# A two-layer decoder trunk on one core: first token loads on ScalarE's queue, squares folded on GpSimd to one product per chunk, and the norm-factor multiply placed behind one weight split

## The chip, the core and the metric

The kernel runs on one core of one Trainium2 chip. A core has five engines with a queue of instructions each, taken strictly in order: TensorE (PE, with its weight loads shown as PEld), VectorE (DVE), ScalarE (ACT), GpSimd (POOL) and SyncE (SP). SP does no arithmetic; it issues DMAs, and so can ACT and POOL. The engines meet only through semaphores. The metric is device time in microseconds for one execution, of which a profile shows one.

## What is computed

Two layers over 256 tokens of width 1024. Each layer is an attention sub-layer followed by a gated ConvFFN, each behind an RMSNorm and added to the residual. Layer 1 mixes three dilated windows (three groups of 16 heads of 64), layer 2 is block-sparse attention, which over 256 tokens is one causal block.

```python
def rmsnorm(x, gain):
    y = xf * lax.rsqrt(jnp.mean(xf * xf, axis=-1, keepdims=True) + RMS_EPS)
    return y * gain

# attention: q and k are normalised per head before rope
q = apply_partial_rope(rmsnorm(qkv[:, :, 0], q_gain), cos, sin)
k = apply_partial_rope(rmsnorm(qkv[:, :, 1], k_gain), cos, sin)
# layer i:
hn = rmsnorm(x, attn_norm[i]); x = x + mixer(hn)
hn = rmsnorm(x, ffn_norm[i]);  x = x + conv_ffn(hn)
```

All inputs are float32. The answer is the sum after the second layer, float32.

## The kernel before

**Tiles and numbers.** Tokens stand in two chunks of 128 (c = 0, 1). A product of float32 precision is made of three products of shortened operands (`mm3`, lines 374 to 376): high part by high part, low by high, high by low. Tokens are split once per norm into `xT` (high and low), weights are split when they arrive.

**The weight stream** (`Stream`, lines 49 to 112). Weights come in units of 512 KB (`raw`, four buffers, loaded by SP). `start` makes the high part of a unit on ACT (`whi`, line 83), `finish` the low part on DVE (`wlo`, line 92) and then issues the load that takes the freed `raw` buffer. The first four units are split in two halves.

**Turns** (line 175). The whole kernel is a list of turns. A turn issues, in this order: `start` for a unit; what stands in the table `first` for this turn; one `finish`; what stands in `pre`; the other `finish`es; the turn's own products on PE, with what stands in `mid` issued half way; what stands in `post`. The call `at(table, dt, fn, ...)` (line 172) enters work for a turn `dt` later. Each engine executes its instructions in the order in which they were issued, so these tables set every engine's order; no scheduler changes it (line 124).

**The first attention.** A `qk_block` for one head group has four parts of 12 products of 512 columns: (c 0, first half of the depth), (c 0, second half), (c 1, first), (c 1, second). In the first section, turns 0 to 3 are the first group's, taken as c 0, c 1, c 0, c 1 (line 651): turns 0 and 1 use units 0 and 1, turns 2 and 3 units 2 and 3, turns 4 and 5 (the second group, c 0) units 4 to 7. When a chunk's part is done, ACT evicts it twice (`sq`, `qk`, lines 422 and 423). One turn later `head_sums` runs: DVE sums the squares by head, POOL makes the factor `rs_y` (`rsqrt_pool`, lines 251 and 253), DVE applies rope. One turn after that `factors` multiplies `qk` by `rs_y` on DVE (line 449), and one turn later PE transposes `qk` (line 465). Attention itself is a chain of steps in later turns: scores on PE (`step_A`), `step_E` (DVE line 582, ACT exponentials line 592), `step_R` (DVE lines 599 and 602 divide `sm`), `step_T` (PE transposes of `sm`, line 609), `step_C` (PE, line 631). A section is four heads of each group; there are four sections.

**The first norm** (`FirstNorm`, line 322). The tokens come already transposed (`x_t`), so the sum of squares over the width runs over partitions. ACT squares two halves of 512 columns, one engine adds the halves (POOL for chunk 0, DVE for chunk 1, line 343), and `sums` (line 345) adds 512 columns by four 128x128 products with a column of ones on PE, which ACT copies to `rn_s` (line 349) and POOL turns into `rn_e` (line 310). `rn_e` goes into every `rs_y` of the chunk.

**The start of the program** (lines 198 to 245 and 820 to 864). SP issues, in this order: `gn` (the gains), half a chunk of tokens, units 0 and 1, two more halves, unit 2, the last half, unit 3, then `pk` (308 KB of packed small tables), then the further units as buffers come free. `gain_tables` (line 231) is 16 small instructions on POOL that read `pk`; it is entered for `post` of turn 0.

Of the kernel before, what the change touches and what calls it, by code (L numbers as in the profile page):

```python
# [17 lines left out]
P = 128  # L18
# [97 lines left out]
def trunk_kernel(ctx, tc, x, a_w_qkv, a_w_o, b_w_qkv, b_w_o, ffn_norm, ffn_w_up, ffn_w_down, gains, pack, mask_a, mask_b,  # L116
                 x_t, out):
    nc = tc.nc
# [51 lines left out]
    first, pre, mid, post = {}, {}, {}, {}  # L170

    def at(table, dt, fn, *args):
        table.setdefault(now[0] + dt, []).append((fn, args))
# [21 lines left out]
        nc.gpsimd.dma_start(g, ffn_norm[l:l + 1, :].to_broadcast([P, D]))  # L195
        return g

    def load_T(c, h):
        nc.sync.dma_start(x_T[c][:, h * 512:(h + 1) * 512], x_t[:, c, h * 512:(h + 1) * 512])

    gn = cp.tile([P, 2, 8], F32, name="gn")
    nc.sync.dma_start(gn, gains.rearrange("p (l k) -> p l k", l=2))
    x_T = [xr[:, c, :] for c in range(2)]
    load_T(0, 0)
    ident = cp.tile([P, P], F32, name="ident")
    make_identity(nc, ident)
    ones = cp.tile([P, 1], F32, name="ones")
    nc.gpsimd.memset(ones, 1.0)
    mhalf = cp.tile([P, 2 * HS], F32, name="mhalf")
    nc.gpsimd.memset(mhalf, -0.5)  # L210
    ws.load(2)
    load_T(1, 0)
    load_T(0, 1)
    ws.load(3)
    load_T(1, 1)
    ws.load(4)


# [29 lines left out]
    def rsqrt_pool(ssq, scale, eps, keep=None):  # L248
        n = ssq.shape[-1]
        v = sp.tile([P, 2 * HS], F32, name="rs_v", bufs=2)[:, 0:n]  # L250
        nc.gpsimd.tensor_scalar(v, ssq, scale, eps, op0=ALU.mult, op1=ALU.add)  # L251
        y = sp.tile([P, 2 * HS], F32, name="rs_y", bufs=4)[:, 0:n] if keep is None else keep
        nc.gpsimd.tensor_tensor(y, v, mhalf[:, 0:n], op=ALU.pow)  # L253
        return y


    class Norm:
# [4 lines left out]
        def square(self, h):  # L262
            junk = sp.tile([P, 512], F32, name="sq", bufs=2)
            nc.scalar.activation(junk, xr[:, self.c, h * 512:(h + 1) * 512], AF.Square,
                                 accum_out=self.acc[:, h:h + 1])
# [56 lines left out]
    class FirstNorm(LateNorm):  # L322
# [15 lines left out]
        def square(self, h):  # L338
            sq = bp.tile([P, 512], F32, name="qk", bufs=4)
            nc.scalar.activation(sq, self.src[:, h * 512:(h + 1) * 512], AF.Square)  # L340
            self.sq.append(sq)
            if h == 1:
                (nc.gpsimd, nc.vector)[self.c].tensor_add(self.sq[0], *self.sq)

        def sums(self):
            acc = ps.tile([P, 512], F32, name="S", bufs=2)[:, 0:1]
            for k in range(4):
                nc.tensor.matmul(acc, self.sq[0][:, k * P:(k + 1) * P], ones, start=(k == 0), stop=(k == 3))
            nc.scalar.activation(self.ssq, acc, AF.Copy)
            self.offset()  # L350

# [27 lines left out]
    def attention(xT, norms, ng, g0, mask):  # L379
# [36 lines left out]
        def qk_block(g, res, rq):  # L416
            res.append(None)

            def done(c, acc):
                qk = bp.tile([P, 512], F32, name="qk", bufs=4)  # L420
                sq = sp.tile([P, 512], F32, name="sq", bufs=2)
                nc.scalar.activation(sq, acc, AF.Square)  # L422
                nc.scalar.activation(qk, acc, AF.Copy)
                at(first, 1, head_sums, c, qk, sq)

            def head_sums(c, qk, sq):
                ssq = sp.tile([P, 8], F32, name="qssq", bufs=2)
                nc.vector.tensor_reduce(ssq, sq.rearrange("p (h d) -> p h d", d=HD), axis=AX.X, op=ALU.add)  # L428
                rs = rsqrt_pool(ssq, 1.0 / HD, norms[c].eps)

                t4 = qk.rearrange("p (j h d) -> p j h d", j=2, d=HD)
                ra = sp.tile([P, 2, HS, 16], F32, name="ra", bufs=1)
                rb = sp.tile([P, 2, HS, 16], F32, name="rb", bufs=1)
                cg = CG[:, c, g0 + g]
                sg = SG[:, c, g0 + g]
                nc.vector.tensor_mul(ra, t4[:, :, :, 0:16], cg[:, :, None, :].to_broadcast([P, 2, HS, 16]))
                for lo_, hi_ in ((0, 8), (8, 0)):
                    nc.vector.tensor_mul(rb[:, :, :, lo_:lo_ + 8], t4[:, :, :, hi_:hi_ + 8],
                                         sg[:, :, None, lo_:lo_ + 8].to_broadcast([P, 2, HS, 8]))
                nc.vector.tensor_add(t4[:, :, :, 0:16], ra, rb)  # L440
                at(first, 1, factors, c, qk, rs)

            def factors(c, qk, rs):

# [199 lines left out]
        for sec in range(NSEC):  # L644
            qk, v, rq = [], [None, None], {}
# [176 lines left out]
    norms = [FirstNorm(xT, c, gn[:, 0], x_T[c], ssq[:, c:c + 1]) for c in range(2)]  # L822
# [10 lines left out]
    def unit():  # L833
        ws.start(1)
        ws.finish(1)
# [7 lines left out]
    norms[0].split(2, 2)  # L843
    unit()
    norms[1].split(0, 4)
    for h in range(2):
        norms[0].square(h)
    norms[0].split(4, 4)

    def second_halves():  # L850
        unit()
        norms[1].split(4, 4)
        unit()
        for h in range(2):
            norms[1].square(h)

    at(post, 0, gain_tables)
    at(mid, 1, second_halves)
    at(mid, 2, norms[0].sums)
    at(mid, 3, norms[1].sums)  # L860
    at(post, 6, factors)
    at(post, 6, nc.sync.dma_start, mA, mask_a)
    at(post, 20, nc.sync.dma_start, mB, mask_b)
# [113 lines left out]
```

## Time and profile before

| | |
|---|---|
| median of 3 runs | 798.68 us (797.98 to 798.79) |
| the profiled execution | 798.67 us, of which the span of the core's instructions is 796.9 us |
| busy | PE 784.2, PEld 688.7, DVE 566.2, ACT 488.3, POOL 101.7 us |
| granted TensorE clock | 0.998 of full speed over the span |

The profile page gives the busy time of each engine, a timeline in slices, the chain of work that ended last, and the costliest groups of instructions. A timeline row gives the start, the duration, the engine, the line, the operation and its tiles; a bracket at its end is the idle time of the engine just before it and what ended it. Rows of pipelined engines overlap by a few hundredths.

### The profile page before, as it was taken

Reading aid. Unit: us, or ns where it says so; the run is one execution under the profiler, and the core shown is the slowest. Engines: PE = TensorE matmul, PEld = TensorE weight load, DVE = VectorE, ACT = ScalarE, POOL = GpSimd, SP = SyncE. Lnnn points to the kernel's source line nnn. Section 1 sums busy time; section 2 is a strip of 40 time slices with the busy share of each in tenths; the row PEclk is TensorE's granted clock in tenths of the full one; section 3 lists DMA queues with packets and bytes.
Section 4 is the critical chain, followed back from the end, with each engine's and each line's share of the span. In section 5 each row is a group of like instructions: output and inputs, shape, how many; then the busy total and the mean of one; then the engine's idle time right before and its main releaser. Section 6 shows DMA issues by size and latency. Waiting matters only on the chain.

```text
span 796.9 us, 13884 instructions
## 1 busy us (share of the span) xinstructions
PE 784.2 (98%) x5298; PEld 688.7 (86%) x5298; DVE 566.2 (71%) x1026; ACT 488.3 (61%) x831; POOL 101.7 (13%) x133
## 2 busy tenths in 40 slices
PE   8999999999999999999999999999999999999997
PEld 6788888888888789999999988788879999999996
DVE  6886786786778466788666776777766687767662
ACT  7578667677677636656555655867755565465550
POOL 3540240241232000000000001221200000000000
PEclk9999999999999999999999999999999999999999
DMA  8676355436446425567665462654525457655631
GB/s 259 194 220 218 107 162 183 132 114 195 143 132 228 143 80 185 159 212 225 198 192 178 159 218 83 202 158 132 169 63 179 146 183 241 212 159 183 204 116 53
DMA packets 111634, 133.93 MB, mean 168 GB/s; under 512 B 5584, under 2 KB 100176, under 8 KB 111568
## 3 DMA queue, kind: packets, MB, share of 16 engines
q1 hardware_dynamic: 110992, 130.96, 52.5%
q0 software_dynamic: 576, 2.10, 0.7%
q8 instruction: 41, 0.67, 0.4%
q14 instruction: 25, 0.20, 0.1%
HBM read 131.99 MB, written 1.05 MB: 167 GB/s over the span
## 4 chain that ended last, share of the span: by engine, by line
PE 89%; ACT 3%; DVE 3%; DMA 1%; POOL 1%; issue 1%; SPq 0%; DVEq 0%; ACTq 0%; POOLq 0%
PE acc L374 12%; PE acc L376 11%; PE acc L375 11%; PE acc L743 10%; PE acc L742 10%; PE acc L741 10%; PE S L782 3%; PE S L783 3%; PE S L784 3%; PE PT L784 2%; PE PT L782 2%; PE PT L783 2%; PE O L631 2%; PE PT L609 2%; PE acc L465 2%; DVE wlo L92 1%
## 5 line engine op out<-in xcount | busy, mean ns | idle before, releaser
L92 DVE TENSOR_TENSOR wlo<-raw,whi 128x1024 fp32r<-128x1024 f32 (+1 forms) x248 | 292.3, 1211 | 80.3 <-ACT whi L83 79.3
L83 ACT ACTIVATE whi<-raw 128x1024 fp32r<-128x1024 f32 (+1 forms) x248 | 249.6, 1039 | 17.8 <-PE PT L783 10.4
L374 PE MATMUL acc<-whi,xT 128*128 128x512 f32 (+1 forms) x544 | 200.3, 368 | 1.6 <-ACT whi L83 1.6
L376 PE MATMUL acc<-wlo,xT 128*128 128x512 f32 (+1 forms) x544 | 193.2, 355 | 2.6 <-DVE wlo L92 2.5
L375 PE MATMUL acc<-whi,xT 128*128 128x512 f32 (+1 forms) x544 | 192.6, 354 | 0.2 <-DVE xT L363 0.2
L743 PE MATMUL acc<-xT,wlo 128*128 128x256 f32 x640 | 181.1, 283 | 0.0
L741 PE MATMUL acc<-xT,whi 128*128 128x256 f32 x640 | 181.1, 283 | 0.0
L742 PE MATMUL acc<-xT,whi 128*128 128x256 f32 x640 | 181.1, 283 | 0.0
L742 PEld LDWEIGHTS acc<-xT,whi 128*128 128x128 f32 x640 | 122.7, 192 | 1.3
L741 PEld LDWEIGHTS acc<-xT,whi 128*128 128x128 f32 x640 | 122.7, 192 | 1.2
L743 PEld LDWEIGHTS acc<-xT,wlo 128*128 128x128 f32 x640 | 122.7, 192 | 0.0
L376 PEld LDWEIGHTS acc<-wlo,xT 128*128 128x128 f32 x544 | 103.1, 189 | 20.1 <-DVE wlo L92 5.5
L374 PEld LDWEIGHTS acc<-whi,xT 128*128 128x128 f32 x544 | 103.2, 190 | 19.2 <-issue 4.1
L375 PEld LDWEIGHTS acc<-whi,xT 128*128 128x128 f32 x544 | 103.3, 190 | 12.9 <-DVE xT L363 0.5
L758 DVE SCALAR_TENSOR_TENSOR qk<-acc,pk,qk 128x255 f32<-128x255 f32 (+1 forms) x160 | 65.9, 474 | 20.2 <-ACT qk L755 20.1
L755 ACT ACTIVATE qk<-acc,pk 128x256 f32<-128x256 f32 x80 | 40.6, 557 | 27.0 <-PE acc L743 27.0
L253 POOL TENSOR_TENSOR rs_y<-rs_v,mhalf 128x8 f32<-128x8 f32 x32 | 53.6, 1674 | 2.7
L767 ACT ACTIVATE kT<-qk 128x512 fp32r<-128x512 f32 x22 | 13.9, 632 | 56.9 <-DVE qk L765 56.9
L251 POOL TENSOR_SCALAR rs_v<-qssq,rn_e 128x8 f32<-128x8 f32 x32 | 14.2, 444 | 216.5 <-DVE qssq L428 216.4
L761 ACT ACTIVATE qk<-qk 128x512 f32<-128x512 f32 x22 | 13.9, 632 | 41.6 <-DVE qk L758 41.6
L422 ACT ACTIVATE sq<-acc 128x512 f32<-128x512 f32 x32 | 19.1, 596 | 26.8 <-PE acc L376 26.5
L449 DVE TENSOR_TENSOR qk<-qk,rs_y 128x512 f32<-128x512 f32 (+1 forms) x32 | 20.1, 629 | 20.6 <-POOL rs_y L253 20.5
(129 smaller groups left out, 987.1 us busy)
## 6 DMA issues: line engine op xcount, KB each, us to landing
raw<-in_ffn_w_up_dram SPq DMA_DIRECT2D x88, 512.0 KB, 4.0
raw<-in_a_w_qkv_dram SPq DMA_DIRECT2D x128, 256.0 KB, 3.8
raw<-in_ffn_w_down_dram SPq DMA_DIRECT2D x44, 512.0 KB, 5.0
raw<-in_b_w_qkv_dram SPq DMA_DIRECT2D x32, 256.0 KB, 4.0
raw<-in_a_w_qkv_dram SPq DMA_DIRECT2D x8, 512.0 KB, 4.8
raw<-in_a_w_o_dram SPq DMA_DIRECT2D x8, 512.0 KB, 4.7
raw<-in_b_w_qkv_dram SPq DMA_DIRECT2D x8, 512.0 KB, 3.8
raw<-in_b_w_o_dram SPq DMA_DIRECT2D x8, 512.0 KB, 3.6
```

The lines of the kernel that those rows point to most:

```text
L83: self.nc.scalar.activation(hi[:, i], raw[:, i], AF.Copy)
L92: self.nc.vector.tensor_sub(lo[:, i], self.raw[self.done][:, i], r32(hi[:, i]))
L253: nc.gpsimd.tensor_tensor(y, v, mhalf[:, 0:n], op=ALU.pow)
L374: nc.tensor.matmul(acc, T[:, k, 0, cs], hi, start=first, stop=False)
L375: nc.tensor.matmul(acc, T[:, k, 1, cs], hi, start=False, stop=False)
L376: nc.tensor.matmul(acc, T[:, k, 0, cs], lo, start=False, stop=last)
L741: nc.tensor.matmul(o, hi[:, k % 4, es], xT[:, k, 0], start=(k == 0), stop=False)
L742: nc.tensor.matmul(o, hi[:, k % 4, es], xT[:, k, 1], start=False, stop=False)
L743: nc.tensor.matmul(o, lo[:, k % 4, es], xT[:, k, 0], start=False, stop=(k == 7))
L755: nc.scalar.activation(o, u, AF.Identity, bias=cw[:, 132 + b:133 + b], scale=cw[:, 88 + b:89 + b])
L758: nc.vector.scalar_tensor_tensor(o[:, d:S], u[:, 0:S - d], cw[:, first_tap + b:first_tap + b + 1], o[:, d:S], op0=ALU.mult, op1=ALU.add)
L782: nc.tensor.matmul(o, acts[f][:, 0, cs], hi[:, sl], start=(b == 0), stop=False)
```

## The change

There are three edits.

1. **Loads.** The first token loads and `gn` are issued by ACT, the first half chunk in two quarters with `gn` between them; the second halves stay on SP. SP begins with weights.
2. **Squares.** After the halves are added, POOL folds the 512 columns to 256 and 128 (for both chunks), and `sums` is one product instead of four. Chunk 0's squares are issued half way through turn 1 instead of ahead of turn 0, and the two `sums` stand at the end of turns 2 and 3 instead of half way through them.
3. **Factor multiply.** `factors` goes from `first` to `pre`: one `finish` (a `wlo` on DVE) is now ahead of it in its turn.

```diff
-    def load_T(c, h):
-        nc.sync.dma_start(x_T[c][:, h * 512:(h + 1) * 512], x_t[:, c, h * 512:(h + 1) * 512])
+    def load_T(e, c, k0, nk):
+        e.dma_start(x_T[c][:, k0 * P:(k0 + nk) * P], x_t[:, c, k0 * P:(k0 + nk) * P])
...
-    nc.sync.dma_start(gn, gains.rearrange("p (l k) -> p l k", l=2))
     x_T = [xr[:, c, :] for c in range(2)]
-    load_T(0, 0)
+    load_T(nc.scalar, 0, 0, 2)
+    nc.scalar.dma_start(gn, gains.rearrange("p (l k) -> p l k", l=2))
+    load_T(nc.scalar, 0, 2, 2)
+    load_T(nc.scalar, 1, 0, 4)
...
     ws.load(2)
-    load_T(1, 0)
-    load_T(0, 1)
+    load_T(nc.sync, 0, 4, 4)
     ws.load(3)
-    load_T(1, 1)
+    load_T(nc.sync, 1, 4, 4)
     ws.load(4)
...
             if h == 1:
-                (nc.gpsimd, nc.vector)[self.c].tensor_add(self.sq[0], *self.sq)
+                a = self.sq[0]
+                (nc.gpsimd, nc.vector)[self.c].tensor_add(a, *self.sq)
+                for w in (256, 128):
+                    nc.gpsimd.tensor_add(a[:, 0:w], a[:, 0:w], a[:, w:2 * w])
...
-            for k in range(4):
-                nc.tensor.matmul(acc, self.sq[0][:, k * P:(k + 1) * P], ones, start=(k == 0), stop=(k == 3))
+            nc.tensor.matmul(acc, self.sq[0][:, 0:P], ones, start=True, stop=True)
...
-                at(first, 1, factors, c, qk, rs)
+                at(pre, 1, factors, c, qk, rs)
...
     norms[1].split(0, 4)
-    for h in range(2):
-        norms[0].square(h)
     norms[0].split(4, 4)
 
     def second_halves():
         unit()
+        for h in range(2):
+            norms[0].square(h)
         norms[1].split(4, 4)
         unit()
...
     at(post, 0, gain_tables)
     at(mid, 1, second_halves)
-    at(mid, 2, norms[0].sums)
-    at(mid, 3, norms[1].sums)
+    at(post, 2, norms[0].sums)
+    at(post, 3, norms[1].sums)
```

Three places show what this does to the engines' orders. The first is POOL at the start of the program; `CG`, `SG` and `gqk` are the tables that `gain_tables` makes from `pk`, and `qk` here holds the squares. Before:

```order
L210 MEMSET mhalf 128x8
L343 TENSOR_TENSOR qk<-qk 128x512
L237 TENSOR_TENSOR CG<-pk 128x96
...
L245 MEMSET gqk 16x4
L310 TENSOR_SCALAR rn_e<-rn_s_108 128x1
L251 TENSOR_SCALAR rs_v<-qssq,rn_e 128x8
```

In the changed kernel:

```order
L213 MEMSET mhalf 128x8
L239 TENSOR_TENSOR CG<-pk 128x96
...
L247 MEMSET gqk 16x4
L346 TENSOR_TENSOR qk<-qk 128x512
L348 TENSOR_TENSOR qk<-qk 128x256
L348 TENSOR_TENSOR qk<-qk 128x128
L348 TENSOR_TENSOR qk<-qk 128x256
L348 TENSOR_TENSOR qk<-qk 128x128
L312 TENSOR_SCALAR rn_e<-rn_s_109 128x1
```

The add of chunk 0's squares stood ahead of the 16 table instructions and now stands behind them, followed by the four folds.

The second is PE from the middle of turn 2 (which is its 31st product of 512 columns on) to the start of turn 3. Before:

```order
L376 MATMUL acc<-wlo,xT 128x512
L348 MATMUL S<-ones,qk 128x1 x4
L374 MATMUL acc<-whi,xT 128x512
L375 MATMUL acc<-whi,xT 128x512
L376 MATMUL acc<-wlo,xT 128x512
```

In the changed kernel, six products on:

```order
L378 MATMUL acc<-whi,xT 128x512
L379 MATMUL acc<-whi,xT 128x512
L380 MATMUL acc<-wlo,xT 128x512
L352 MATMUL S<-ones,qk 128x1
L378 MATMUL acc<-whi,xT 128x512
```

The sum over partitions is one product instead of four, and all 36 products of turns 0 to 2 stand ahead of it; every product of turn 3 stands behind it.

The third is a place in the second section of the first attention, which the third and the fourth section repeat: on DVE the split of keys (`kL`, `kT`), a weight split, the division of `sm` and the next chunk's head sums, and on PE the transposes of `qk` and `sm` that follow. On DVE, before:

```order
L507 TENSOR_TENSOR kT<-acc,kT 64x2x128
L92 TENSOR_TENSOR wlo<-raw,whi 128x1024
L599 RECIPROCAL rd<-den 128x2
L602 TENSOR_SCALAR sm<-sm,rd 128x384 x2
L428 TENSOR_REDUCE qssq<-sq 128x8
```

On DVE in the changed kernel:

```order
L511 TENSOR_TENSOR kT<-acc,kT 64x2x128
L92 TENSOR_TENSOR wlo<-raw,whi 128x1024
L453 TENSOR_TENSOR qk<-qk,rs_y 128x512
L603 RECIPROCAL rd<-den 128x2
L606 TENSOR_SCALAR sm<-sm,rd 128x384 x2
L432 TENSOR_REDUCE qssq<-sq 128x8
```

On PE at the end of the same turn, before:

```order
L375 MATMUL acc<-whi,xT 128x512
L376 MATMUL acc<-wlo,xT 128x512
L465 MATMUL acc<-ident,qk 128x128 x4
L609 MATMUL PT<-ident,sm 128x128 x6
L374 MATMUL acc<-whi,xT 128x512
```

On PE in the changed kernel:

```order
L379 MATMUL acc<-whi,xT 128x512
L380 MATMUL acc<-wlo,xT 128x512
L613 MATMUL PT<-ident,sm 128x128 x6
L469 MATMUL acc<-ident,qk 128x128 x4
L378 MATMUL acc<-whi,xT 128x512
```

The factor multiply moved from a place further up (ahead of the masks and maxima of line 582) to between the weight split and the division of `sm`, and since `step_T` is now entered ahead of the transposes of `qk`, PE takes the transposes of `sm` first.

## Rows read from the trace of the kernel before

**Rows 1.** The page, part 1: busy time, share of the span, instructions.

```profile
PE 784.2 (98%) x5298; PEld 688.7 (86%) x5298; DVE 566.2 (71%) x1026; ACT 488.3 (61%) x831; POOL 101.7 (13%) x133
```

**Rows 2.** Busy time by stretch: length, engines' busy us (instructions), granted clock, DMA share, GB/s.

```profile
7.20:10.00 2.80, 2.78 (x9) 1.46 (x10) 2.75 (x6) 2.73 (x7) 0.00 (x0) 1.00 1.08 377
...
26.00:30.00 4.00, 2.02 (x9) 1.21 (x8) 3.50 (x9) 0.74 (x1) 2.35 (x3) 0.97 0.34 113
30.00:33.30 3.30, 3.30 (x12) 2.78 (x11) 2.94 (x8) 3.03 (x7) 1.50 (x2) 0.52 0.78 239
```

**Rows 3.** Timeline of SP, start of the program: start, us, line, what is loaded.

```profile
0.73 0.39 SPq L202 DMA_DIRECT2D gn<-in_gains_dram  x1
1.17 0.42 SPq L199 DMA_DIRECT2D xr<-in_x_t_dram  x1
...
8.74 0.34 SPq L220 DMA_DIRECT2D pk<-in_pack_dram  x1
```

**Rows 4.** Timeline of POOL, 11 to 22 us: the add of squares and the tables.

```profile
11.85 1.30 POOL L343 TENSOR_TENSOR qk<-qk 128x512 f32<-128x512 f32 x1 [10.46 <-ACT qk L340]
14.62 0.93 POOL L237 TENSOR_TENSOR CG<-pk 128x96 f32<-128x96 f32 x1 [1.47 <-DMA pk<-in_pack_dram]
...
16.10 0.44 POOL L237 TENSOR_TENSOR CG<-pk 128x96 f32<-128x96 f32 x1
...
16.79 0.73 POOL L240 TENSOR_TENSOR SG<-pk 128x48 f32<-128x48 f32 x1
...
19.93 0.24 POOL L237 TENSOR_TENSOR CG<-pk 128x32 f32<-128x32 f32 x1
...
21.28 0.10 POOL L245 MEMSET gqk<- 16x4 f32 x1
```

**Rows 5.** Timeline of DVE, 16 to 29 us: weight splits and the first factor multiply.

```profile
16.61 1.46 DVE L92 TENSOR_TENSOR wlo<-raw,whi 128x512 fp32r<-128x512 f32 x2
...
25.49 0.69 DVE L449 TENSOR_TENSOR qk<-qk,rs_y 128x512 f32<-128x512 f32 x1 [1.94 <-POOL rs_y L253]
...
27.56 1.22 DVE L92 TENSOR_TENSOR wlo<-raw,whi 128x1024 fp32r<-128x1024 f32 x1
```

**Rows 6.** Timeline of PE, 15 to 30 us: sums, two neighbouring products, the last stall.

```profile
15.78 0.95 PE L348 MATMUL S<-ones,qk 128*128 128x1 f32 x8
...
18.24 0.39 PE L376 MATMUL acc<-wlo,xT 128*128 128x512 f32 x1
...
25.11 0.39 PE L375 MATMUL acc<-whi,xT 128*128 128x512 f32 x1
...
25.34 0.39 PE L376 MATMUL acc<-wlo,xT 128*128 128x512 f32 x1
...
28.84 0.50 PE L376 MATMUL acc<-wlo,xT 128*128 128x512 f32 x1 [1.98 <-DVE wlo L92]
...
29.64 0.54 PE L376 MATMUL acc<-wlo,xT 128*128 128x512 f32 x1
```

**Rows 7.** Timeline of DVE in the second section, 87 to 94 us.

```profile
87.32 0.68 DVE L449 TENSOR_TENSOR qk<-qk,rs_y 128x512 f32<-128x512 f32 x1
...
89.96 0.48 DVE L509 SCALAR_TENSOR_TENSOR kL<-acc,gqk,kT 64x256 fp32r<-64x256 f32 x1 [0.80 <-ACT kT L501]
...
93.18 0.75 DVE L602 TENSOR_SCALAR sm<-sm,rd 128x384 f32<-128x384 f32 x2
```

**Rows 8.** Timeline of PE at the same place, 93 to 95 us.

```profile
93.72 0.60 PE L465 MATMUL acc<-ident,qk 128*128 128x128 f32 x4
94.16 0.82 PE L609 MATMUL PT<-ident,sm 128*128 128x128 f32 x6
94.73 0.48 PE L374 MATMUL acc<-whi,xT 128*128 128x512 f32 x1
```

**Rows 9.** Timeline of DVE and PE in the second layer's attention, 503 to 514 us.

```profile
503.14 0.42 DVE L449 TENSOR_TENSOR qk<-qk,rs_y 128x256 f32<-128x256 f32 x1
...
513.56 0.50 PE L560 MATMUL S<-kT,t 64*128 64x256 f32 x4 [0.99 <-DVE t L507]
```

## The prediction

> **What bounds the kernel now.** PE is busy for 784 of 797 us [rows 1], so what happens on other engines counts only where PE waits for it, and a wait of PE is paid in full: nothing later has slack to give it back. I therefore read the busy times by engine first, then the list of waits for the places where PE sits idle, then the timeline around them. The one large loss that lies near an edited line is at the start. At 28.84 PE resumes after almost 2 us on a weight split of DVE [rows 6]. That split had been queued behind the first factor multiply, which itself waited 1.94 us for POOL's `rs_y` [rows 5], and POOL was late because its tables waited for `pk` until 14.62 and ended at 21.38 [rows 4]. Behind the stall, PE's granted clock falls to half: 0.52 of full speed from 30.0 to 33.3, and 0.97 in the stretch ahead of it [rows 2]. That is 3.3 x 0.48 = 1.6 us plus 0.1, so 1.7 us lost. The chain thus runs from the landing of `pk` over the tables to PE, and every edit has to be held against it.
>
> **Loads.** No instruction is added; issues go from SP to ACT, which has nothing to do then but its table load. Their worth at the start of PE (some 0.4 to 1 us, from the first token load that SP issued at 1.17, behind `gn` at 0.73 [rows 3]) will be hidden, as the next part shows. What counts is when `pk` lands. Ahead of it on SP stood 13 DMAs, now 10, and SP issued it at 8.74 [rows 3], so about 8.0 / 13 = 0.6 us per DMA. If issue were the limit, it would land 3 x 0.6 = 1.8 us earlier. But the bytes ahead of it are the same, and the DMA engines are busy without a gap at that time (share 1.08 [rows 2]). Then only the earlier start is won, 1.17 - 0.73 = 0.44 us. So POOL can begin its tables between 12.8 and 14.2; I take 13.7, nearer to the end that the DMA share supports.
>
> The Trainium skill, in "DMA: Bandwidth & Descriptors" (section "Issuing engines are not separate DMA queues"), says that DMAs of several engines share the same 16 DMA engines and that issuing from more of them saves issue time alone. The DMA share in that row agrees. By that rule `pk` would come at 14.2 and the whole sum below would end 0.5 us higher, at 802.4.
>
> **Squares.** On PE it removes six products with a column of ones. The eight records of four products take 0.95 us [rows 6], so one product costs 0.24 and the two sums cost 0.48 instead of 1.9: 1.4 us won. On POOL, the add of chunk 0's squares, which took 1.30 us while POOL was still waiting for `pk` [rows 4], now stands behind the 16 table instructions, and two folds follow it. That adds a wait to PE, which takes its instructions in order: the product with the ones at the end of turn 2 needs the folded squares, and all of turn 3 is queued behind it. When are they there? The tables took 21.38 - 14.62 = 6.8 us. Part of that is DVE: beside a weight split at 16.61 [rows 5] a table of 48 columns took 0.73, while one of 96 columns without one took 0.44 [rows 4]. Six of the 16 at 0.44 and ten at 0.24 (the row at 19.93) are 5.0 us, the lower end. The splits run beside them as before, so I keep 6.8. The add takes 1.30; from 0.44 at 96 columns and 1.30 at 512, a column costs 2.1 ns, so the fold to 256 takes 0.77 and to 128 takes 0.51: 2.6 us together. Chunk 0's sum is ready at 13.7 + 6.8 + 2.6 = 23.1, between 12.8 + 5.0 + 2.6 = 20.4 and 24.6 (14.2 for `pk`, and 1.0 more if splits lie beside the adds too).
>
> PE gets there much sooner. Before, the 36th product started at 18.24, with 1 us of sums and two short stalls ahead of it [rows 6]; now it ends by about 17.5. So PE stands for some 5.5 us. ACT stands too: its copy of the sum is queued ahead of the splits of units 5 and 6. The gain at the start and the faster sums vanish in this wait.
>
> From 23.1 on: one sum, 12 products of turn 3, one sum, 24 of turns 4 and 5, at 0.23 each (25.11 to 25.34 [rows 6]): 0.24 + 2.76 + 0.24 + 5.52 = 8.8, so turn 5 ends at 31.9. Chunk 1's folds, 1.3 us behind chunk 0's, are done long before turn 3 is. Before, turn 5's last product starts at 29.64 [rows 6] and is through at 29.87. The old stall is gone in this: the split of unit 7 no longer waits for `rs_y`, and with ACT released at about 23.5, units 5 to 7 are split about 1 us ahead of PE's need. The clock loss of 1.7 us, which before followed an idle time of 2 us, I expect again behind one of 5.5 us, so it cancels; its bounds are none and two such stretches. **The start costs 31.9 - 29.9 = +2.0 us** (-0.7 to +3.5, and 1.7 either way for the clock). It breaks even where the folded squares are ready at 21.1.
>
> **Factor multiply.** It moves one instruction of DVE per chunk and head group and takes away most waits of DVE on `rs_y`; DVE is not the bound, so this alone is worth nothing behind the start. But it changes two other things. In the second section of the first attention, the multiply (0.68 us [rows 7]) leaves its place ahead of the maxima and now stands between a weight split and the division of `sm`. The maxima come earlier, but the split of keys behind them waits for ACT until 89.96 either way [rows 7], so the division, at 93.18, comes 0.6 to 0.7 later: its first half is done at about 93.8 + 0.4 = 94.2. PE now wants the transposes of `sm` first, at 93.72, where it used to do those of `qk` (0.44 us [rows 8]) while the division ended. So it waits about 0.5 us, does 0.57 of `sm` and 0.44 of `qk`, and reaches the next product at 95.2 instead of 94.73. The pattern repeats in the third and the fourth section: **3 x 0.5 = +1.5 us**, between nothing (if ACT releases the keys sooner) and 1.9. At the other swapped places the division is done in time. In the second layer the multiply at 503.14 (0.42 us) leaves the chain of maxima, exponentials and splits that ends in PE's wait of 0.99 at 513.56 [rows 9]: between 0 and -0.4, I take **-0.3**, since the transposes that used to fill the earlier wait now follow it.
>
> **Sum.** Against the profiled execution (798.67, practically the median of 798.68): 798.67 + 2.0 + 1.5 - 0.3 = **801.9 us**.
>
> **Rivals.** *A wash*: the tables meet fewer splits and the folded squares are ready at about 21, so the start costs nothing, and the division in the three sections is not late. Then 798.67 + 0.3 - 0.3 = 798.7. For it: the lower end of the tables, 5.0 us; against it: the splits that fall beside them are the same ones. *Faster*: PE does not wait at the sum at all. The point is 17.5: if the folded squares are there by then, the 1.4 us of products, the 2.0 of the old stall and its 1.7 of clock are all won, 5.1 us, and with the sections the time is 798.67 - 5.1 + 1.2 = 794.8. It needs `pk` at 17.5 - 2.6 - 5.0 = 9.9, where SP had only issued it at 8.74 [rows 3] and it landed 5.9 later. *Costlier*: behind the longer idle time PE runs a second stretch at half clock, 801.9 + 1.7 = 803.6. Against it: before, one stretch was enough though PE was fed no better.
>
> **How the numbers follow.** The forecast has 0.53, costlier 0.12, the wash 0.27, faster 0.08. A measurement of this kernel tells about 0.2%, 1.6 us, from no change. Of the wash 0.05 lies beyond that bound on the fast side, 0.20 within it and 0.02 beyond it on the slow side, and of the forecast's own lower end 0.05 lies within; so faster 0.13, same 0.25, slower 0.62. The range leaves out the fast rival and the far ends of the tables and the clock: 798.0 to 804.2.
>
> **What would show it.** In the changed profile POOL's first instruction after its memsets is a table, near 13.7, and the fold of 128 columns ends near 23. PE has an idle time of 4 to 6 us ahead of the product with the ones, put down to POOL; the granted clock is near 0.5 for some 3 us around or behind it; the wait for a weight split near 28 is gone. In the second to fourth section PE waits about half a microsecond for the division of `sm`, put down to DVE. I am wrong if POOL begins its tables near 10, if PE's wait at the first sum is under 3 us, or if no wait for the division shows.

## The result, and the profile of the changed kernel

The changed kernel takes 804.13 us in the median (803.55 to 806.39, 4 runs) against 798.64 for the kernel before on the same chip (4 runs). The ratio on record is 1.0079, 95% interval 1.0067 to 1.0091; the two medians give 1.0069, the two means 1.0076. It is slower, as forecast, but by 5.5 us in the median where I had 3.2. The median lies just inside the range of 798.0 to 804.2; by the ratio on record the time would be about 805, above it. Its profiled execution took 803.73 us with a span of 802.0, against 798.67 and 796.9 before: 5.1 us more in the span. One execution of all those below, of the kernel with loads and split tables, took 2679.86 us and counts as slow, and its ratio leaves it out.

The page's first part, busy time by engine, against [rows 1]:

```profile
PE 784.9 (98%) x5286; PEld 689.9 (86%) x5286; DVE 565.0 (70%) x1026; ACT 487.4 (61%) x831; POOL 94.8 (12%) x137
```

PE has 12 records fewer (six products with the ones, two records each) and is busy for 0.7 us more. So the 5.1 us are for the most part idle time. PE's waits (who waited, for whom: us in total, times, longest):

```profile
PE S L352 <- POOL qk L348: 4.8, 1, 4.8
PE PT L613 <- DVE sm L606: 2.4, 4, 1.0
...
PE acc L380 <- DVE wlo L92: 0.8, 1, 0.8
```

The wait on `wlo` that stood at 28.84 [rows 6] is gone. A wait of 4.8 us on POOL's folded squares and three new waits for the division of `sm` are there. The timeline of POOL, against [rows 4]:

```profile
13.07 0.39 POOL L239 TENSOR_TENSOR CG<-pk 128x96 f32<-128x96 f32 x1 [11.68 <-DMA pk<-in_pack_dram]
...
19.27 1.26 POOL L346 TENSOR_TENSOR qk<-qk 128x512 f32<-128x512 f32 x1
20.61 2.54 POOL L348 TENSOR_TENSOR qk<-qk 128x256 f32<-128x256 f32 x4
```

and of PE, against [rows 6]:

```profile
16.76 0.39 PE L380 MATMUL acc<-wlo,xT 128*128 128x512 f32 x1
21.99 0.59 PE L352 MATMUL S<-ones,qk 128*128 128x1 f32 x2 [4.84 <-POOL qk L348]
22.43 0.77 PE L378 MATMUL acc<-whi,xT 128*128 128x512 f32 x1
...
27.96 0.48 PE L378 MATMUL acc<-whi,xT 128*128 128x512 f32 x1
...
32.63 0.39 PE L380 MATMUL acc<-wlo,xT 128*128 128x512 f32 x1
...
44.52 0.50 PE L380 MATMUL acc<-wlo,xT 128*128 128x512 f32 x1 [0.79 <-DVE wlo L92]
```

The tables begin at 13.07 and run in one piece to 19.2, the add follows, and the first two folds end near 21.9. PE, ready at 17.1, stands until then. `pk`, whose landing the tables waited for, was issued by SP, against [rows 3]:

```profile
8.23 0.47 SPq L222 DMA_DIRECT2D pk<-in_pack_dram  x1
```

That is 0.51 us earlier than before; the first table is 1.55 us earlier.

The windows view (length, busy time of each engine, granted clock, DMA share, GB/s), against [rows 2]:

```profile
21.20:27.90 6.70, 5.91 (x16) 4.76 (x16) 3.83 (x6) 2.07 (x3) 4.90 (x7) 0.50 0.32 106
28.00:30.00 2.00, 2.00 (x10) 1.65 (x11) 1.33 (x5) 2.00 (x5) 0.64 (x3) 1.00 0.79 202
30.00:36.00 6.00, 6.00 (x30) 4.97 (x29) 5.08 (x10) 3.23 (x8) 2.38 (x3) 1.00 0.60 179
```

From 21.2, still in the wait, to 27.9 PE has 0.50 of its clock, the 1.2 GHz level; the half-clock stretch of before, 30.0 to 33.3 in [rows 2], is gone.

Since both kernels multiply the same products with weights in the same order, I count them and compare the start of the same product in both traces. This turns a difference of 5.1 us into places:

| product with weights, and what stands there | before | after | later by |
|---|---|---|---|
| first | 7.21 | 6.82 | -0.39 |
| last ahead of the wait at the sum | 18.24 | 16.76 | -1.48 |
| first behind it | 18.47 | 22.43 | 3.96 |
| first behind the second sum, where the half clock ends | 22.14 | 27.96 | 5.82 |
| the one that stalled before [rows 6] | 28.84 | 32.63 | 3.79 |
| behind the half clock of before | 32.97 | 35.14 | 2.17 |
| where PE waits anew for `wlo` | 41.53 | 44.52 | 2.99 |
| behind the division of the fourth section | 221.59 | 226.39 | 4.80 |
| second layer, behind PE's wait of [rows 9] | 514.79 | 519.21 | 4.42 |
| second layer, 64 us on | 578.03 | 583.19 | 5.16 |

In words: 1.5 us ahead; then 5.4 lost at the wait and 1.9 more to the half clock (less the second sum's products); 2.0 and 1.6 come back where before had its stall and its half clock; 0.8 lost at 44.5; 1.8 in the sections; 0.4 won and 0.7 lost in the second layer.

### The profile page after: what moved, and what is told of

Same layout as the page of the kernel before. It is cut to its first block, busy times and chain, and to the rows that moved or that the text cites. A ratio compares the mean times of both kernels' runs of the same rounds, so it can differ in the third digit from the quotient of the medians.

```text
span 802.0 us, 13858 instructions
## 1 busy us (share of the span) xinstructions
PE 784.9 (98%) x5286; PEld 689.9 (86%) x5286; DVE 565.0 (70%) x1026; ACT 487.4 (61%) x831; POOL 94.8 (12%) x137
## 4 chain that ended last, share of the span: by engine, by line
PE 83%; DVE 6%; ACT 6%; issue 2%; DMA 1%; POOL 1%; ACTq 0%; DVEq 0%; SPq 0%; POOLq 0%
PE acc L378 10%; PE acc L747 10%; PE acc L746 10%; PE acc L745 10%; PE acc L379 9%; PE acc L380 9%; PE S L786 3%; PE S L787 3%; PE S L788 2%; PE PT L786 2%; PE PT L788 2%; PE PT L787 2%; DVE wlo L92 2%; PE O L635 2%; ACT sm L596 2%
## 5 line engine op out<-in xcount | busy, mean ns | idle before, releaser
L762 DVE SCALAR_TENSOR_TENSOR qk<-acc,pk,qk 128x255 f32<-128x255 f32 (+1 forms) x160 | 66.0, 475 | 21.3 <-ACT qk L759 21.2
L759 ACT ACTIVATE qk<-acc,pk 128x256 f32<-128x256 f32 x80 | 40.5, 556 | 27.6 <-PE acc L747 27.6
L771 ACT ACTIVATE kT<-qk 128x512 fp32r<-128x512 f32 x22 | 13.9, 632 | 57.0 <-DVE qk L769 57.0
L765 ACT ACTIVATE qk<-qk 128x512 f32<-128x512 f32 x22 | 13.9, 632 | 41.9 <-DVE qk L762 41.8
L786 PE MATMUL S<-whi,kT 128*128 128x512 f32 x88 | 34.7, 394 | 0.0
```

The lines of the kernel that those rows point to most:

```text
L759: nc.scalar.activation(o, u, AF.Identity, bias=cw[:, 132 + b:133 + b], scale=cw[:, 88 + b:89 + b])
L762: nc.vector.scalar_tensor_tensor(o[:, d:S], u[:, 0:S - d], cw[:, first_tap + b:first_tap + b + 1], o[:, d:S], op0=ALU.mult, op1=ALU.add)
L786: nc.tensor.matmul(o, acts[f][:, 0, cs], hi[:, sl], start=(b == 0), stop=False)
```

## The experiments

Two questions were open: which edit loses what, and whether the start's loss is the order of POOL's queue (theory M; P, a wider form of it, comes from the run with the tables behind the folds), the loads and the clock (rival R), or the squares' later place in itself (rival Q). The runs come from several chips, on which the kernel before has medians of 798.2 to 798.6, so differences between kernels below are good to some tenths of a us. Median, and the ratio on record to the kernel before on the same chip:

| kernel | median, us | ratio (95%) |
|---|---|---|
| loads alone | 797.25 | 0.9989 (0.9980 to 0.9998) |
| squares alone | 802.57 | 1.0059 (1.0046 to 1.0071) |
| factor alone | 799.07 | 1.0010 (1.0001 to 1.0019) |
| loads and squares | 801.92 | 1.0044 (1.0031 to 1.0057) |
| all three | 804.13 | 1.0079 (1.0067 to 1.0091) |
| all, tables behind the folds | 803.01 | 1.0061 (1.0049 to 1.0074) |
| all, transposes back ahead | 801.87 | 1.0046 (1.0033 to 1.0058) |
| loads, squares, split tables | 800.62 | 1.0027 (1.0018 to 1.0035) |
| the same, squares early | 799.54 | 1.0018 (1.0009 to 1.0027) |
| the same, query gain early | 798.76 | 1.0007 (0.9999 to 1.0016) |
| loads, split tables | 796.73 | 0.9984 (0.9975 to 0.9993) |
| loads, split tables, query gain early | 795.09 | 0.9962 (0.9950 to 0.9975) |
| the same, one head sum behind a split | 795.32 | 0.9965 (0.9951 to 0.9978) |

### Each edit by itself

**Loads alone** (edit 1 on the kernel before).

> The kernel before with the loads of the first tokens alone on the activation engine's queue. Theory M: the first product starts 0.4 us earlier, the tables 0.9 to 1.5 us earlier, and the wait at 28.84 us becomes 1 to 1.5 us shorter: 797.2 to 798.4. Rival R (TensorE at half clock until 10.9 us costs what it shows): 799 to 801.

797.25 us: the gain is there, at the fast end of M's range, and R is out by nearly 2 us. Its trace, of PE:

```profile
28.03 0.50 PE L378 MATMUL acc<-wlo,xT 128*128 128x512 f32 x1 [1.99 <-DVE wlo L92]
...
40.06 0.50 PE L378 MATMUL acc<-wlo,xT 128*128 128x512 f32 x1 [0.80 <-DVE wlo L92]
```

M's mechanism was only half right: the stall of 28.84 comes 0.8 us earlier, but is as long as before. In this trace no half clock follows it, and a new wait of 0.80 stands at 40.06, on the same product as the one at 44.52 in the changed kernel. So that wait does not come from the factor.

R named the slow first products. In the changed kernel they stand 0.43 us apart up to 10.83, as in its half-clock stretch, and 0.23 apart behind. They stand so here too (6.92 to 10.33) and with the squares alone (7.21 to 10.62), whose loads are those of before, but not with loads, split tables and early query gain (7.78 to 8.71, 0.23 apart). So they do not come from the loads, and the changed kernel reaches the wait at the sum 1.5 us ahead all the same.

**Squares alone** (edit 2 on the kernel before).

> The kernel before with the squares' edit alone (their later place, the folds on GpSimd, one product per chunk); loads and factor as before. Theory P (the tables and then the folds stand in GpSimd's queue ahead of the sum and of the first norm factor): TensorE waits 4 to 5.5 us at the sum as in the changed kernel and runs at half clock behind it; with the loads of before nothing is gained ahead of it: 802 to 803.5, as the loads with the squares (801.9) or up to 1.1 above, the gain of the loads. Rival (the two edits only clash together, the early loads against the late squares): 798 to 800.

802.57 us, inside P's range. PE's wait at the sum is 6.1 us, longer than expected:

```profile
23.52 0.59 PE L350 MATMUL S<-ones,qk 128*128 128x1 f32 x2 [6.07 <-POOL qk L346]
```

Loads alone (-1.1) and squares alone (+4.4) add up to +3.3; together they were measured at +3.6. So the two do not clash; the squares lose and the loads make a little of it good.

**Loads and squares** (the changed kernel with the factor back).

```diff
-                at(pre, 1, factors, c, qk, rs)
+                at(first, 1, factors, c, qk, rs)
```

> The changed kernel with the norm-factor multiply back ahead of the weight split; loads and folded squares stay. Theory M: the three sections give back 0.65 us each, the wait of 0.8 us at 44.5 us and 0.4 us of the second layer go as well, 3.1 in all: 800.5 to 801.5. A wait of the kind that stood at 28.84 us in the kernel before (1.98 us) may come back and take up to 2 of it: then 803. Rival R (all of the loss is made in the first 30 us): within 0.5 us of 804.1.

801.92 us: 0.4 above M's range and 2.2 below the changed kernel, so the factor carries that much of the loss, and R, which put all of it into the first 30 us, falls. (Its one trace is only 1.3 us below, since PE's wait at the sum is 5.42 us there; with the same start, the kernel with the transposes back ahead has 5.33 and the changed kernel 4.84.) The waits of PE from 500 to 600 us, first of the changed kernel, then of this one:

```profile
PE PT L613 <- DVE sm L606: 1.0, 1, 1.0
PE S L564 <- DVE t L511: 0.6, 1, 0.6
PE S L552 <- ACT t L505: 0.4, 1, 0.4
PE O L635 <- ACT pT L620: 0.3, 1, 0.3
```

```profile
PE S L564 <- DVE t L511: 1.0, 1, 1.0
PE PT L613 <- DVE sm L606: 0.8, 1, 0.8
```

The two waits on ACT (PE goes on at 553.5 and 582.6 us) belong to the factor too. One expectation failed: the wait at 44.5 did not go with the factor. It stands here at 45.35, 0.79 us long, and M had put it down to the wrong edit.

**Factor alone** (edit 3 on the kernel before).

> The kernel before with the norm-factor multiply alone placed behind one weight split. Theory M: three times 0.65 us at the transposes and 0.8 us at 44.5 us are added, and up to 2.0 us at 28.84 us come back, since there the split's low part stood behind the factor: between 798.6 + 0.8 = 799.4 and 798.6 + 3.1 = 801.7. Rival R (this edit only gains, the first 30 us of the other edits lose): 796.6 to 798.6.

799.07 us, just under M's lower end and over R's upper. In its trace the stall of 28.84 is gone, as reckoned, and PE, 0.5 us behind the kernel before just ahead of that place, is 3.2 us ahead of it once the half clock of before is over: 2.1 come from the stall and 1.6 from the half clock, which does not come here. But at 40.5 only 1.0 is left:

```profile
38.10 0.63 PE L465 MATMUL acc<-ident,qk 128*128 128x128 f32 x4 [0.67 <-DVE qk L449]
...
40.54 0.50 PE L376 MATMUL acc<-wlo,xT 128*128 128x512 f32 x1 [1.35 <-DVE wlo L92]
```

The sections and the second layer then take 2.1 us, against 2.2 in the changed kernel. So behind the start the edit has the same price in both traces, and what it wins at the start depends on what else is late there.

### The factor: the swap of the transposes

```diff
-                at(post, 1, transpose, c, qk)
+                post.setdefault(now[0] + 1, []).insert(0, (transpose, (c, qk)))
```

> The changed kernel with the four transposes of a q/k block put back ahead of the transposes of the softmax at each place where the later factor had swapped them; the factor stays behind the split. If the swap makes TensorE's wait at L613 (0.85 us at 97.35 us, three times) because it leaves nothing to do there, the four transposes, some 0.45 us, fill it: 3 times 0.4 to 0.65 us less, 801.8 to 802.9. If the later softmax division on VectorE alone sets it, the wait stands at other instructions and the time stays at 803.6 to 804.6.

801.87 us, as much as taking the factor edit back. The changed kernel at the second section, DVE and then PE, against [rows 7] and [rows 8]:

```profile
94.85 1.23 DVE L92 TENSOR_TENSOR wlo<-raw,whi 128x1024 fp32r<-128x1024 f32 x1
95.99 0.68 DVE L453 TENSOR_TENSOR qk<-qk,rs_y 128x512 f32<-128x512 f32 x1
...
96.78 0.75 DVE L606 TENSOR_SCALAR sm<-sm,rd 128x384 f32<-128x384 f32 x2
```

```profile
96.50 0.39 PE L380 MATMUL acc<-wlo,xT 128*128 128x512 f32 x1
97.35 0.85 PE L613 MATMUL PT<-ident,sm 128*128 128x128 f32 x6 [0.46 <-DVE sm L606]
98.03 0.60 PE L469 MATMUL acc<-ident,qk 128*128 128x128 f32 x4
98.39 0.48 PE L378 MATMUL acc<-whi,xT 128*128 128x512 f32 x1
```

and PE with the transposes ahead again:

```profile
96.42 0.63 PE L469 MATMUL acc<-ident,qk 128*128 128x128 f32 x4
96.89 0.85 PE L613 MATMUL PT<-ident,sm 128*128 128x128 f32 x6
97.50 0.48 PE L378 MATMUL acc<-whi,xT 128*128 128x512 f32 x1
```

The four transposes fill the time in which DVE still divides, and the waits in the three sections are gone though the division is as late as in the changed kernel (in this trace it starts at 96.39, 0.09 behind the point where PE's last product makes way). The later multiply alone costs nothing in the sections (this kernel is 2.5 us behind the kernel before at 44 us and again at 239); that it also moved the transposes, which are entered one turn after it, did. In the second layer this kernel keeps the two waits on ACT.

### The start: POOL's queue

**Tables behind the folds** (all three edits).

```diff
-    at(post, 0, gain_tables)
+    at(post, 1, gain_tables)
```

> The changed kernel with the gain tables one turn later, so that GpSimd has them behind the squares' sum and folds. Theory M (GpSimd's order is the start's cost: in the changed kernel the sum of the first squares stands behind tables that end at 19.18 us, and TensorE idles 4.8 us at L352 before 21.99 and then runs at half clock until 27.95): the wait at the sum goes, 4 to 6 us come back at that place, and 1 to 3 us of them are lost again because the tables now end near 24.5 instead of 19.2 and the first norm factors with them; 798.5 to 801. Rival R (the first products at half clock until 10.9 us, from the loads on the activation queue, or the clock by itself, made the loss): 803 to 805, the wait gone but the time with it elsewhere.

803.01 us: in numbers a miss for M and at the lower end of R's range. The trace shows that the loss is not at the first products, where R put it (PE is 0.4 us ahead of the kernel before at the end of turn 2), and why M missed. PE no longer waits at the sum, but the first `rs_y` is late instead. POOL, then DVE:

```profile
26.33 0.94 POOL L312 TENSOR_SCALAR rn_e<-rn_s 128x1 f32<-128x1 f32 x1
27.39 0.27 POOL L253 TENSOR_SCALAR rs_v<-qssq,rn_e 128x8 f32<-128x8 f32 x1
27.74 1.68 POOL L255 TENSOR_TENSOR rs_y<-rs_v,mhalf 128x8 f32<-128x8 f32 x1
```

```profile
29.45 0.69 DVE L453 TENSOR_TENSOR qk<-qk,rs_y 128x512 f32<-128x512 f32 x1 [2.22 <-POOL rs_y L255]
...
33.18 0.69 DVE L453 TENSOR_TENSOR qk<-qk,rs_y 128x512 f32<-128x512 f32 x1 [1.90 <-POOL rs_y L255]
```

The first factor multiply is at 29.45, against 25.49 in [rows 5]. I had looked at one customer of POOL. It has three in a row, the folded squares, the tables and the `rs_y`, and PE is held by whichever stands last. PE now waits 1.70 us at the transposes of `qk` that the late multiply feeds (30.20), and a half-clock stretch follows. That is theory P, and it says that the order alone cannot repair the start: either work leaves POOL's queue, or work that is not yet needed goes behind `rs_y`.

**Split tables**: six of the twelve table instructions and the query gain (`gqk`) serve later work. In the kernel with loads and squares:

```diff
-        for tab, m0, m1 in ((tabs[0], 0, 6), (tabs[1], 6, 8)):
+        for tab, m0, m1 in ((tabs[0], 0, 6), (tabs[1], 6, 8))[l:l + 1]:
...
+        if l == 0:
+            return
         nc.gpsimd.tensor_mul(gqk, gcol[:, 0, :], gcol[:, 1, :])
...
-    at(post, 0, gain_tables)
+    at(post, 0, gain_tables, 0)
+    at(post, 4, gain_tables, 1)
```

> The changed kernel with the factor ahead of the split and with the gain tables in two parts: the first layer's six operations where they were, the second layer's and the query gain three turns later. Theory P (GpSimd is one queue of some 10 us of work ahead of the first norm factor, and whatever stands last in it holds TensorE): the squares' sum is ready 4 us earlier, near 18, and the first norm factors are not held by the tables either; TensorE idles under 1 us at the sum: 795.5 to 797.5. Rival Q (the squares' own place, later on the activation engine and on GpSimd, costs by itself, whatever stands beside them): 799 to 801.5.

800.62 us, 1.3 below loads and squares, but 3 us over P's range and in Q's. PE still waits 3.4 us at the sum (20.46). POOL, then DVE:

```profile
16.62 1.27 POOL L348 TENSOR_TENSOR qk<-qk 128x512 f32<-128x512 f32 x1
17.96 3.74 POOL L350 TENSOR_TENSOR qk<-qk 128x256 f32<-128x256 f32 x4
```

```profile
16.65 1.79 DVE L348 TENSOR_TENSOR qk<-qk 128x512 f32<-128x512 f32 x1
```

The folds now meet DVE's work on SBUF. DVE's add of chunk 1's squares took 0.68 us in the kernel with late tables, where POOL stood idle; here, begun 0.03 us behind POOL's add, it took 1.79, and the four folds took 3.74 against 2.54 in the changed kernel. The Trainium skill, in "SBUF — State Buffer" (section "Who interferes with whom"), says that a VectorE instruction with two SBUF inputs contends with a GpSimd instruction that reads SBUF, and that the port they share is an exclusive lock. The first pair of numbers agrees with it: DVE's add ends 0.55 us behind POOL's, near the 0.68 that it takes alone. The second goes the same way.

**Squares early**: chunk 0's squares back ahead of the last split, so that POOL does them while it waits for `pk`; first with the query gain in the late part of the tables, then in the early one (the first two changed lines are of the second kernel alone).

```diff
-        if l == 0:
+        if l == 1:
             return
...
     norms[1].split(0, 4)
+    for h in range(2):
+        norms[0].square(h)
     norms[0].split(4, 4)
...
         unit()
-        for h in range(2):
-            norms[0].square(h)
         norms[1].split(4, 4)
```

> As the kernel with split tables, and the first chunk's squares back at their place ahead of the last weight split, so that on GpSimd the first chunk's sum and folds stand ahead of the tables and the second chunk's folds behind the first layer's six. Theory P: both sums are ready when TensorE comes to them, as with the split alone: 795.5 to 797.5. Rival Q: only this kernel is rid of the loss, 1.5 us or more below the kernel with split tables.

> The loads, split tables, early query gain, and the folded squares at their early place: all that the changed kernel's start has, in a better order on GpSimd. Theory P: the second chunk's folds (2.44 us on GpSimd, ending at 21.1 us) still stand ahead of the first norm factor, VectorE waits 1.9 us for it and TensorE 1 to 2.4 us behind: 797.8 to 799.0, and 2 to 3 us above the same kernel without folds. Rival (the folds cost nothing once the order is right): within 0.5 us of the kernel without folds, 795.2 to 796.2.

799.54 and 798.76 us. The first missed both expectations: 2 us over P's range, and only 1.1 below the kernel with split tables where Q asked for 1.5. The second is inside P's. PE does not wait at the sums in either; in the first it waits for `wlo` twice, 2.39 us at 28.83 and 2.28 at 42.33, of which the early query gain takes the second away (0.20). Of the second kernel, POOL, then DVE and PE:

```profile
18.88 2.37 POOL L350 TENSOR_TENSOR qk<-qk 128x256 f32<-128x256 f32 x2 [1.55 <-DVE qk L348]
21.33 1.25 POOL L314 TENSOR_SCALAR rn_e<-rn_s 128x1 f32<-128x1 f32 x1
22.68 1.12 POOL L255 TENSOR_SCALAR rs_v<-qssq,rn_e 128x8 f32<-128x8 f32 x1
23.89 1.68 POOL L257 TENSOR_TENSOR rs_y<-rs_v,mhalf 128x8 f32<-128x8 f32 x1
```

```profile
25.60 0.69 DVE L455 TENSOR_TENSOR qk<-qk,rs_y 128x512 f32<-128x512 f32 x1 [1.94 <-POOL rs_y L257]
```

```profile
28.95 0.79 PE L382 MATMUL acc<-wlo,xT 128*128 128x512 f32 x1 [2.44 <-DVE wlo L92]
```

Everything is in the best order I found, and chunk 1's two folds, which wait 1.55 us for DVE's add and then take 2.37, still stand ahead of the first `rs_y`, PE's stall of [rows 6] is back, and the kernel cannot be told from the one before.

**Loads and split tables, without the folds**: squares, sums and factor as before; first with the query gain late, then early.

> The kernel before with the loads on the activation engine's queue and the gain tables in the same two parts; squares, sums and factor as before. Theory P: the first norm factor, for which VectorE waits 1.94 us at 24.68 us with the loads alone, comes 2 us earlier, TensorE's wait of 2.0 us at 28 goes, and up to 1 us of it is lost again to VectorE's chain ahead of 40 us: 795.3 to 796.3. Rival (that chain on VectorE is what counts, the wait ahead of it is slack): 797.0 to 797.5, no change from the loads alone.

> The loads with split tables, the query gain now in the first part. With it in the second part the activation engine waits 1.29 us at 29.45 us for it and VectorE's chain up to the split at 38.07 us starts as much later. Theory P: that comes back, 795.2 to 796.0. Rival (a later bound makes it good): 796.4 to 797.0 as with the gain in the second part.

796.73 and 795.09 us, the first between P's range and its rival's, the second 0.1 below P's. In the first, ACT waited for the query gain in the late part, which the second moves:

```profile
29.45 0.47 ACT L505 ACTIVATE kT<-acc,gqk 64x256 fp32r<-64x256 f32 x1 [1.29 <-POOL gqk L248]
```

In the second, of POOL and of DVE:

```profile
20.26 1.73 POOL L257 TENSOR_TENSOR rs_y<-rs_v,mhalf 128x8 f32<-128x8 f32 x1
```

```profile
22.65 0.68 DVE L453 TENSOR_TENSOR qk<-qk,rs_y 128x512 f32<-128x512 f32 x1
```

The first `rs_y` is 3.6 us earlier than with the folds, DVE does not wait for it, and PE's stall near 28 is gone. The two kernels differ in the folds and in the sums behind them alone (one product at the end of a turn against four half way through it): 798.76 against 795.09. So the folds cost 3.7 us even with the squares at their early place and POOL in the better order, more than the 2 to 3 that P named; in that trace a half-clock stretch follows the stall (28.7 to 32.1). Q is thus not needed for most of the loss. What the later place alone costs, without folds, was not tried. This is also the fastest kernel of the study, 0.38% below the kernel before (0.25 to 0.50).

**One head sum behind a split**, for the wait of `wlo` near 40:

```diff
-                at(first, 1, head_sums, c, qk, sq)
+                at(pre if dil and now[0] == 7 and g == 1 and c == 1 else first, 1, head_sums, c, qk, sq)
```

> The loads with split tables and early query gain, and in one turn the head sums (reduction, rotation; 1.4 us on VectorE) behind the first weight split, for whose end TensorE waits 2.27 us at 39.34 us. Theory P (VectorE's chain is the bound there): 0.8 to 1.4 us less than without, 794.0 to 795.2. Rival (the low parts that follow then come late instead): the same as without, 795.2 to 796.0.

795.32 us: nothing, as the rival said. The first low part comes earlier, PE then waits 0.9 us for the next one.

Of P's seven forecasts two hold in numbers (squares alone; squares with early query gain). What the traces show of it is the mechanism: wherever the folds stand in POOL's queue, PE's longest wait of the first 31 us goes back to POOL, at the sum or, by way of DVE, at `rs_y`. How much comes back when a place in that queue is freed, P could not tell.

## Why the prediction was wrong in size

**What held.** The direction, and the two causes that carry the loss. POOL's first instruction is a table at 13.07 (forecast 13.7, bounds 12.8 and 14.2); PE's idle time at the first sum is 4.8 us, put down to POOL (4 to 6); the stall near 28 is gone; PE waits for the division in sections two to four. I had read the rule of the Trainium skill that I cited ("DMA: Bandwidth & Descriptors", section "Issuing engines are not separate DMA queues") as a landing at 14.2; it was 13.07. The trace splits the 1.55 us: SP issued `pk` 0.51 earlier, close to the 0.44 that I had for the start and far from the 1.8 of three issues less, so the saving of issue time agrees with the rule. The other 1.0 us is the transfer, 4.8 us from issue to the first table against 5.9, which neither of my two bounds had a term for; why it was shorter was not tried. In the traces of all runs the first table stands between 13.1 and 13.9 where it waits for `pk` of the new loads, and between 14.6 and 15.2 with the loads of before.

**The start, +2.0.** At the place where the half clock of before ends, the traces show +2.17, so the sum came out, but two of its terms were wrong and offset each other. The folded squares were there at 21.9, 1.2 us sooner than the 23.1 I had. And the half-clock stretch was not like that of before, 3.3 us, but 6.7 (the "costlier" rival, which I gave 0.12): the last product of turn 5 made way at 33.5, 11.6 us behind the squares, where I had 8.8. Of these 2.8 us, 1.6 came back where before had its own stretch; I had let the two cancel. The 1.2 us left over is just what the squares were early by, and that is luck.

**The step that failed: what is late next.** I let the clock loss of before cancel in full, and did not ask what would end last behind turn 5 once its stall and its half clock were gone. It is DVE's chain of key evictions, head sums and splits. From the product at 32.97 (35.14 after) to the one at 41.53 (44.52 after), which needs the chain's last split, it takes 9.4 us where PE waits: 9.38 in the changed kernel, 9.41 with the loads alone. Before, PE itself needed 8.56 and came just as the split was done. PE and DVE before, then DVE in the changed kernel:

```profile
41.53 0.50 PE L376 MATMUL acc<-wlo,xT 128*128 128x512 f32 x1
```

```profile
40.25 2.36 DVE L92 TENSOR_TENSOR wlo<-raw,whi 128x1024 fp32r<-128x1024 f32 x2
```

```profile
43.25 3.69 DVE L92 TENSOR_TENSOR wlo<-raw,whi 128x1024 fp32r<-128x1024 f32 x3
```

The first of these splits ends some 1.2 us behind its start, near 41.5 before and 44.5 after, where PE goes on. So the chain had no slack left, and half of the 1.6 us that the missing half-clock stretch gives back is lost again, 0.8 us. My sum had no term for it. The runs show the same wait with and without the factor. My rows stopped at 30 us.

**The sections, +1.5.** The mechanism was right, the term too small: 0.65 each (3.00 to 3.66, 3.59 to 4.25 and 4.15 to 4.80 in the difference of starts), 1.8 net. The division begins as late as I had it, 0.05 behind the point where PE's last product makes way (neighbouring products start 0.23 us apart, though a row is 0.39 long: 96.50 + 0.23 = 96.73). But I let PE start 0.4 us into the division, and it starts 0.57 in (97.35 against 96.78).

**The second layer, -0.3.** At the place I priced, the gain is there: 0.34 (4.77 to 4.43 in the difference of starts). I did not look at the other places where the multiply moves in that layer. At the two new waits on ACT 0.7 is lost, so the term was +0.4 and not -0.3.

Together 0.2 + 0.8 + 0.3 + 0.7 make 2.0, the 1.9 us by which the span missed the sum. That is the account of the traced run, 803.73. The slowest of the four, 806.39, also has the lowest granted clock (0.993 against 0.996); no trace of it is kept, so what cost it stays open. The wash, to which I gave 0.27, needed the folded squares at 21.1; they came at 21.9, close to it, and the time still went the other way, for the clock and the other terms above.

**What the edits are worth.** Loads -1.1 us, squares +4.4, factor +2.2 on top of them and +0.7 alone. The six products that edit 2 saves on PE are worth 1.4 us at most, and it pays for them with 2.5 to 3.7 us of folds on an engine that is busy for 12% of the run and on which PE's start hangs from 13 to 24 us.

## What to carry to other kernels

An engine's share of busy time over the whole run says nothing of a start: list everything that stands in its queue ahead of the first result that the bottleneck engine needs, and move work there only if all its customers still get theirs in time. What moves out of the queue instead (here tables for a later layer) can be worth more than the change under study. When a stall or a slow clock is reckoned to vanish, price the next chain behind it up to the point where it ends, and when an instruction moves by a turn, follow what is entered relative to it: here it was the transposes, and not the multiply, that cost time.

## What the runs showed of the hardware that I had not expected

At idle times of PE of 3.4 to 6.1 us at the sum (five kernels), the clock fell to half while PE still stood, for 6.7 to 6.8 us each time. At idle times near 2 us it differed: half for 3.4 us in the kernel before (1.98 us idle), with tables behind the folds (1.70), with early squares and early gain (2.44) and with loads and split tables (2.27), but full with the loads alone (1.99) and with early squares and late gain (2.39 and 2.28). The time differs between runs of one kernel along with it: loads and split tables took 796.4 to 796.7 us in the runs with a mean clock of 0.999 or 1.000, and 797.3 to 798.1 in those at 0.997 or 0.998, while the kernel with the query gain early, whose longest wait on a split is 0.8 us, stayed within 795.08 to 795.27. What decides it behind 2 us was not tried.

The first product with weights started at 7.21 in the trace of before, and at 6.62 and 6.32 in two kernels with the loads of before (squares alone, factor alone). So what the loads seem to win there (0.4 us in the changed kernel's trace, 0.9 with the loads alone) is within what that start varies by; that they win 1.1 us rests on the timed runs.
